# Transformer block on one NeuronCore: the rows of w_down multiplied by the gate g2 beside the up projection, through DRAM

## Chip, cores and metric

The kernel runs on one core of one Trainium2 chip. The metric is the device time of one execution in microseconds. Three runs of the kernel before gave 1492.29, 1489.33 and 1492.66 us; their median is 1492.29 us.

The engines are named as in the profile: PE is the matrix engine, DVE the vector engine, ACT the scalar engine, POOL is GpSimd, and SP is the engine whose queue starts the DMAs of this kernel.

## The reference

One diffusion block over 1024 tokens of width 1024. With `c` the conditioning row, the part that matters here is

```
sh1, sc1, g1, sh2, sc2, g2 = split(silu(c) @ w_mod + b_mod, 6)
h = rms_norm(x, norm1) * (1 + sc1) + sh1
x = x + g1 * (neighbourhood_attention(h, ...) @ w_o)
h = rms_norm(x, norm2) * (1 + sc2) + sh2
a, g = split(h @ w_up, 2)                       # 1024 -> 2 x 2816
x = x + g2 * ((a * gelu(dwconv3(g) + conv_b)) @ w_down)   # 2816 -> 1024
```

The gate `g2` is a row of 1024 numbers, one for each output column. So `g2 * (act @ w_down)` is the same as `act @ (w_down * g2)`, and the kernel uses the second form: every row of `w_down` is multiplied by `g2`, element by element, before it is used. Everything is fp32. Each fp32 matrix product is made of three products of a reduced type: an operand is split into a high part (a copy by ACT) and a low part (the operand minus the high part, by DVE or POOL), and high x high, high x low and low x high are summed.

## The kernel before

Attention and the output projection fill roughly the first 820 us of the span. Behind them come the two stages of the feed-forward part.

**Up projection** (from about 820 to 1240 us). `w_up` and the tokens are cut into 2 x 2 blocks and multiplied in seven products in place of eight. The loop runs over 11 pairs of feature blocks, `i` = 0 to 10, each with `part` 1 (the gate branch `g`, PSUM banks `pg`) and `part` 0 (the value branch `a`, banks `pa`); both share the bank `sw`. Each part has seven steps, `op` in the order 1, 2, 5, 6, 7, 3, 4, so there are 11 x 2 x 7 = 154 steps, and each step is 12 matmuls of 128x512 (line 740). The operand of a step is made ahead of it by `prep_up` (lines 678 to 691): ACT copies the high part (L687) and POOL subtracts it for the low part (L688); this runs `UA` = 6 steps ahead of PE. The raw blocks `ur` come by DMA (L667) and DVE forms their sums (L673 to L675, L686). The banks are emptied by ACT (L772) and DVE (L760, L762, L774, L766); the convolution taps are on DVE (L787). `finish` (L799 to L809) sends the gated rows `y` and four sums of them, `sa` and `sb` (DVE, L804 to L807), to `act_dram`.

**Down projection** (from about 1240 us to the end). It has the same seven products, over 11 blocks `c` in groups of 2, 3, 3 and 3. `load_raw` (L853 to L863) brings two blocks of 128 rows of `w_down` into SBUF as tiles `dr{c}_0` and `dr{c}_1` (L861) and multiplies each by `g2b`, the gate row copied to all partitions: the block with `m` = 0 on POOL, that with `m` = 1 on DVE (L862, 128x1024 each). That makes 22 loads of 512 KB, 11 products on POOL and 11 on DVE. `prep_b` forms the block sums on DVE (L887, L889, L891, L893) and splits the results (ACT L895; POOL or DVE L896). `prep_a` loads the gated rows `da` from `act_dram` (L869) and splits them (ACT L870; POOL or DVE L871). `down_mm` runs the matmuls (L909 to L911) in the banks `dtr`, `dpq`, `dpo` and `dx`, which are the banks that the up projection used, and DVE adds each result to its accumulator (L914). The accumulators start as the residual rows.

**What sets the order.** Each engine executes its instructions in a fixed order, and so does the DMA queue of SP. The program's order is not taken as written: a scheduler orders every engine's instructions by a simulated timeline. It mixes work of the down projection into the end of the up projection: the loads `dr` of group 0 stand on SP's queue ahead of the last `act_dram` stores, and the products and block sums of `dr` stand on POOL and DVE between the splits and taps of the last two feature pairs. `tc.issue_after(x)` holds an instruction back in that order until `x` has been placed, and adds no wait.

**Buffers.** `dr` tiles lie in the eight buffers that the `ur` tiles used (tag x1) and in six others (tag wa). `g2b` is loaded at the end of the first feature pair (L833 to L835), into the buffer of the first `ur` tile.

Of the kernel before, what the change touches and what calls it, by code (L numbers as in the profile page):

```python
# [10 lines left out]
F32 = mybir.dt.float32  # L11
F32R = mybir.dt.float32r
AF = mybir.ActivationFunctionType
ALU = mybir.AluOpType
# [4 lines left out]
P = 128  # L19
D = 1024  # L20
# [10 lines left out]
NF = DFF // P  # L31
# [5 lines left out]
HALF = 512  # L37
# [13 lines left out]
NA = ()  # L51
WD, SQD = range(8), ()
LAG = 1
DG = (1,)
HP_ = (3, 5, 6)
RL = 6
WORD = (1, 2, 5, 6, 7, 3, 4)
DORD = (2, 1, 5, 6, 3, 7, 4)

# [2 lines left out]
def block_kernel(ctx, tc, x, ctxt, cc, w_mod, b_col, b_row, n1, n2, w_qkv, gains, rpb_t, mask_i, mask_r, w_o,  # L62
                 w_up, conv_w, conv_b, w_down, comb, out):
    nc = tc.nc
    PE, ACT, DVE, POOL, SP = nc.tensor, nc.scalar, nc.vector, nc.gpsimd, nc.sync
# [11 lines left out]
    def f(ap):  # L77
        return ap.bitcast(F32)
# [5 lines left out]
    dram = ctx.enter_context(pool("dram", space=DRAM))  # L84
# [22 lines left out]
    o_dram = dram.tile([NPAIR, P, SEQ], F32, name="o_dram")  # L107
    g_dram = dram.tile([2, D], F32, name="g_dram")
    x1_dram = dram.tile([NB, P, D], F32, name="x1_dram")
    act_dram = dram.tile([NF // 2, P, 7, HALF], F32, name="act_dram")  # L110

    big = ctx.enter_context(pool("big", side="right"))
# [43 lines left out]
        DVE.tensor_scalar(ss, ss, 1.0 / D, EPS, ALU.mult, ALU.add)  # L156
        POOL.tensor_tensor(ss, ss, mhalf[:, 0:1], ALU.pow)

    # adaLN of the attention branch, normalised and modulated tokens, transposed and split
    att = ExitStack()  # L160
    sa = att.enter_context(pool("sa"))

# [106 lines left out]
            if si == 3:  # L269
                DVE.tensor_tensor(b1, pc[:, 1], bcol[:, 0:8].unsqueeze(2).broadcast_to([P, KC, 2]), ALU.add)  # L270

    # attention, with the projections of the next pair of heads in between
    sb = att.enter_context(pool("att"))
    mi = sb.tile([P, 3 * P], F32, name="mi")
    SP.dma_start(out=mi, in_=mask_i)
# [179 lines left out]
        DVE.tensor_tensor(res[a:b], po[a:b], tmp[a:b], ALU.add)  # L455
        SP.dma_start(out=o_dram[p, a:b, u * 2 * P:(u + 1) * 2 * P], in_=res[a:b])

    # adaLN of the rest, a little at a time
    def mod_gen():
        order = [2, 3, 4, 5]  # L460
        for sgi in order:
# [27 lines left out]
                        DVE.scalar_tensor_tensor(dst, dst, 1.0, n2c[:, nk * hf:nk * (hf + 1)], ALU.add, ALU.mult)  # L489
                yield  # L490

    # output projection: its first half runs beside the attention of the last heads
    xpool = ctx.enter_context(ExitStack())
    x1, wo, g1b, xsb = {}, [], [], []
    HP = NPAIR // 2
# [106 lines left out]
    filler(10 ** 6)  # L602
    att.close()

    # rest of the output projection, second norm, operands of the Winograd form (seven products of halves
    # in place of eight) of the up projection: A is w_up^T in 2 x 2 blocks, B the tokens in 2 x 2 blocks
    ff = ctx.enter_context(ExitStack())
    usb = ff.enter_context(pool("ffn"))
    BT = {}
    btags = ["bA"] * 12 + ["bB"] * 10 + ["wa"] * 6  # L610
    for i, op in enumerate(WORD):
        for j in range(4):
            tag = btags[4 * i + j]
# [3 lines left out]
            else:  # L617
                BT[op, hl, kk] = usb.tile([P, 2, HALF], F32R, tag=tag, bufs=12 if tag == "bA" else 10,
                                          name=f"b{op}{hl}{kk}")
# [26 lines left out]
            ACT.activation(h, r, AF.Copy)  # L646
            (POOL if op in HP_ else DVE).tensor_tensor(l, r, f(h), ALU.subtract)

    # up projection, gate with the token convolution; the gated rows and their sums go out for the down projection
    NP2 = NF // 2  # L650
    lo_, hi_ = slice(0, HALF), slice(HALF, SEQ)
    uraw, uop = {}, {}
    parts = [(i, part) for i in range(NP2) for part in (1, 0)]
    useq = [(0, 1, 1), (0, 1, 2), (0, 0, 1), (0, 0, 2)] + [(0, part, op) for part in (1, 0) for op in WORD[2:]]
    useq += [(i, part, op) for i, part in parts[2:] for op in WORD]
# [22 lines left out]
    def prep_up(i, part, op):  # L678
        if (i, part) == (0, 1) and op in (1, 2):
            s = xslot(f"u{i}_{part}_{op}", F32R)  # L680
        else:
            s = slot(("rh", "rl")[cnt[0] % 2], f"u{i}_{part}_{op}", shape=(P, 2, HALF))
            cnt[0] += 1
        r = uraw[i, part]
        if op == 3:
            DVE.tensor_tensor(r[3], r[2], r[6], ALU.subtract)  # L686
        ACT.activation(s[:, 0], r[op], AF.Copy)  # L687
        POOL.tensor_tensor(s[:, 1], r[op], f(s[:, 0]), ALU.subtract)  # L688
        uop[i, part, op] = s
        if op == 4 and parts.index((i, part)) + 2 < len(parts):  # L690
            raw_up(*parts[parts.index((i, part)) + 2])
# [107 lines left out]
    def finish(i, y):  # L799
# [8 lines left out]
        SP.dma_start(out=act_dram[i, :, 3:5, :], in_=sa_)  # L808
        SP.dma_start(out=act_dram[i, :, 5:7, :], in_=sb_)  # L809

    sw = ps.tile([P, SEQ], F32, tag="s", bufs=1, name="sw")
    late_p1 = usb.tile([P, HALF], F32, name="late_p1")
    nprep, gens, g, y, late = 2, {}, {}, {}, []
    for k, (i, part, op) in enumerate(useq):
        while nprep < min(k + 1 + UA, len(useq)):
            prep_up(*useq[nprep])
            nprep += 1
        if (i, part) not in gens:
            if part:
                g[i] = [slot("wx", f"g{i}_{m}", F32) for m in range(2)]  # L820
                y[i] = [slot("t4", f"y{i}_{m}", F32) for m in range(2)]
            gens[i, part] = up_part(i, part, g[i] if part else y[i])
        next(gens[i, part])
        if op == WORD[-1]:
            if part:
                for m in range(2):
                    conv(2 * i + m, g[i][m], y[i][m])
                for o, p in late:
                    DVE.tensor_tensor(o, p, o, ALU.mult)
                late.clear()  # L830
            else:
                finish(i, y[i])
                if i == 0:  # L833
                    g2b = slot("gb", "g2b", F32)
                    SP.dma_start(out=g2b, in_=g_dram[1:2, :].broadcast_to([P, D]))  # L835

    # down projection, also in seven products; rows of w_down scaled by the gate g2
    xt = ps.tile([P, 2, HALF], F32, tag="s", bufs=1, name="dx")
    tr = [ps.tile([P, HALF], F32, tag="tr", bufs=3, name=f"dtr{j}") for j in range(3)]
    pq = [ps.tile([P, HALF], F32, tag="pq", bufs=2, name=f"dpq{j}") for j in range(2)]  # L840
# [12 lines left out]
    def load_raw(c):  # L853
        for m in range(2):
            if rt[0] % 14 < 8:
                r = xsb[0].tile([P, D], F32, tag="x1", bufs=NB, name=f"dr{c}_{m}")
            else:
                r = slot("wa", f"dr{c}_{m}", F32)
            rt[0] += 1
            fc = 2 * c + m  # L860
            SP.dma_start(out=r, in_=w_down[fc * P:(fc + 1) * P, :])  # L861
            (DVE if m in DG else POOL).tensor_tensor(r, r, g2b, ALU.mult)  # L862
            raws[c, m] = r  # L863

    def prep_a(q):
# [114 lines left out]
```

## Time and profile before

| quantity | value |
|---|---|
| median of three runs | 1492.29 us (1489.33 to 1492.66) |
| span of the profiled execution | 1491.8 us |
| PE busy | 1386.5 us (93%), 7396 matmuls |
| DVE busy | 1208.1 us (81%) |
| POOL busy | 805.7 us (54%) |
| ACT busy | 738.1 us (49%) |
| moved by DMA | 153.27 MB, 103 GB/s over the span |

The profile is of one execution, for which the trace gives the span, from its first to its last instruction, of 1491.8 us; no separate time of that execution is given, and the span lies 0.5 us below the median of the runs. A row of a group reads: line, engine, operation, tile written <- tiles read, shape, count | busy us, mean ns of one | idle us of its engine just before, and whose end that idle time waited for. A row of the timeline begins with its start and its length in us, and ends with the idle time before it and its releaser in brackets. In a table of stretches, x is the number of instructions, and PEclk the clock that the throttle granted PE, 1.00 being full. Busy shares are averages over stages; which engine is late is read stage by stage.

### The profile page before, as it was taken

The numbers are of one execution on the slowest core, as the hardware profiler recorded it, in microseconds if no ns is written. First come the engines' busy times: TensorE is split into PE (matmuls) and PEld (weight loads), VectorE is DVE, ScalarE is ACT, GpSimd is POOL, SyncE is SP. The second block draws the span as 40 slices with busy tenths as digits, with TensorE's granted clock in tenths as the row PEclk, the third lists the DMA queues.
The fourth block names the chain that finished last, engine by engine and source line by source line (L and its number), as shares of the span: only waits on it lengthen the run. The fifth ranks groups of instructions, "written<-read, shape, count | busy, mean of one in ns | idle before, by whom it ended". The sixth has DMA issues, their size and how long they took to land.

```text
span 1491.8 us, 22077 instructions
## 1 busy us (share of the span) xinstructions
PE 1386.5 (93%) x7396; PEld 1200.0 (80%) x7396; DVE 1208.1 (81%) x2392; ACT 738.1 (49%) x1601; POOL 805.7 (54%) x672
## 2 busy tenths in 40 slices
PE   6689999999999999999996999999999987898998
PEld 2589889898989899888885777888888865686887
DVE  6778878888888878866589889788877779988884
ACT  6575645555565656645465434344343334244541
POOL 1455544545454546744368545555545568474872
PEclk9899999999999999999997999999999998899999
DMA  9612221313131202262132132233332347433343
GB/s 315 161 37 60 64 87 55 92 51 103 49 101 45 77 14 73 69 152 76 50 129 99 64 108 101 96 106 106 107 106 99 106 137 286 155 100 127 110 131 105
DMA packets 84827, 153.27 MB, mean 103 GB/s; under 512 B 9945, under 2 KB 49001, under 8 KB 84713
## 3 DMA queue, kind: packets, MB, share of 16 engines
q1 hardware_dynamic: 84712, 151.86, 32.7%
q8 instruction: 58, 0.95, 0.3%
q14 instruction: 57, 0.46, 0.1%
HBM read 119.05 MB, written 32.78 MB: 102 GB/s over the span
## 4 chain that ended last, share of the span: by engine, by line
PE 60%; DVE 20%; DMA 7%; POOL 5%; issue 4%; ACT 3%; SPq 0%; DVEq 0%; POOLq 0%; ACTq 0%
PE pg L740 8%; PE pa L740 7%; PE sw L740 6%; PE pq L301 5%; PE pq L303 5%; PE pq L305 5%; DMA mr<-in_w_mod_dram 2%; DVE y L787 2%; DVE p L410 2%; POOL u L688 2%; PE s L398 2%; PE po L448 2%; PE po L449 2%; PE py L525 2%; PE py L526 2%
## 5 line engine op out<-in xcount | busy, mean ns | idle before, releaser
L688 POOL TENSOR_TENSOR u<-ur,u 128x512 fp32r<-128x512 f32 x154 | 231.9, 1519 | 176.8 <-ACT u L687 175.1
L417 POOL TENSOR_TENSOR p<-p,m 128x640 f32<-128x640 f32 (+1 forms) x128 | 157.3, 1230 | 157.0 <-DVE m L413 116.0
L301 PE MATMUL pq<-wh,hth 128*128 128x384 f32 (+1 forms) x640 | 219.7, 343 | 17.1 <-DVE kn L340 15.3
L305 PE MATMUL pq<-wh,htl 128*128 128x384 f32 (+1 forms) x640 | 215.2, 336 | 2.4 <-DVE htl L194 1.4
L303 PE MATMUL pq<-wl,hth 128*128 128x384 f32 (+1 forms) x640 | 215.0, 336 | 0.5 <-POOL wl L147 0.5
L687 ACT ACTIVATE u<-ur 128x512 fp32r<-128x512 f32 x154 | 93.9, 628 | 116.1 <-PE sw L740 45.4
L412 ACT ACTIVATE p<-p,m 128x640 f32<-128x640 f32 (+1 forms) x128 | 102.9, 804 | 84.3 <-DVE m L410 75.2
L301 PEld LDWEIGHTS pq<-wh,hth 128*128 128x128 f32 x640 | 124.8, 195 | 23.1 <-DVE kn L340 9.2
L325 POOL TENSOR_TENSOR qss<-qss,mhalf 128x4 f32<-128x4 f32 (+1 forms) x80 | 79.9, 999 | 97.0 <-DVE qss L324 82.8
L305 PEld LDWEIGHTS pq<-wh,htl 128*128 128x128 f32 x640 | 124.7, 195 | 3.2 <-DVE htl L194 3.2
L303 PEld LDWEIGHTS pq<-wl,hth 128*128 128x128 f32 x640 | 124.8, 195 | 1.6 <-issue 0.9
L787 DVE SCALAR_TENSOR_TENSOR y<-g,cw,y 128x896 f32<-128x896 f32 (+1 forms) x132 | 102.8, 842 | 19.2 <-ACT y L781 19.1
L449 PE MATMUL po<-pt,v 128*128 128x256 f32 x352 | 93.3, 293 | 2.1 <-DVE pt L437 2.1
L448 PE MATMUL po<-pt,v 128*128 128x256 f32 x352 | 93.8, 289 | 0.1
L895 ACT ACTIVATE db<-dr 128x512 fp32r<-128x512 f32 x77 | 47.4, 629 | 87.3 <-PE dx L911 55.7
L871 POOL TENSOR_TENSOR da<-da 128x512 fp32r<-128x512 f32 x44 | 74.9, 1725 | 27.4 <-ACT da L870 27.4
L896 POOL TENSOR_TENSOR db<-dr,db 128x512 fp32r<-128x512 f32 x44 | 64.9, 1494 | 45.6 <-ACT db L895 34.3
L410 DVE CUSTOM_DVE_ANT_0 p<-s,bias 128x640 f32<-128x640 f32 x96 | 78.3, 816 | 9.5 <-PE s L399 8.9
L436 ACT ACTIVATE pt<-pl 128x384 fp32r<-128x384 f32 (+1 forms) x128 | 58.0, 461 | 47.6 <-PE pl L429 46.6
L471 DVE SCALAR_TENSOR_TENSOR macc<-mr,cs,macc 128x256 f32<-128x256 f32 x112 | 65.0, 581 | 13.9 <-DMA mr<-in_w_mod_dram 13.0
L437 DVE TENSOR_TENSOR pt<-pl,pt 128x384 fp32r<-128x384 f32 (+1 forms) x128 | 65.4, 516 | 6.7 <-ACT pt L436 6.2
L449 PEld LDWEIGHTS po<-pt,v 128*128 128x128 f32 x352 | 66.6, 189 | 4.0 <-DVE pt L437 3.4
(258 smaller groups left out, 4184.3 us busy)
## 6 DMA issues: line engine op xcount, KB each, us to landing
ur<-in_w_up_dram SPq DMA_DIRECT2D x44, 512.0 KB
da<-act_dram SPq DMA_DIRECT2D x77, 256.0 KB
mr<-in_w_mod_dram SPq DMA_DIRECT2D x128, 128.0 KB
dr<-in_w_down_dram SPq DMA_DIRECT2D x22, 512.0 KB
wraw<-in_w_qkv_dram SPq DMA_DIRECT2D x56, 192.0 KB
mraw<-in_w_mod_dram SPq DMA_DIRECT2D x16, 512.0 KB
act_dram<-sa SPq DMA_DIRECT2D x11, 512.0 KB
act_dram<-y SPq DMA_DIRECT2D x11, 512.0 KB
```

The source lines that it names most:

```text
L301: PE.matmul(pq[:, c0:], hth[t][:, k, :], wh[:, c0:], start=(k == 0), stop=False)
L303: PE.matmul(pq[:, c0:], hth[t][:, k, :], wl[:, c0:], start=False, stop=False)
L305: PE.matmul(pq[:, c0:], htl[t][:, k, :], wh[:, c0:], start=False, stop=(k == KC - 1))
L410: DVE.tensor_tensor_reduce(out=dst, in0=src, in1=bb, scale=1.0, scalar=3e38, op0=ALU.add, op1=ALU.min, accum_out=m[:, 0:1])
L412: ACT.activation(w[:, :n], w[:, :n], AF.Exp, bias=m[:, 0:1], scale=-1.0, accum_out=m[:, 1:2])
L417: POOL.tensor_tensor(w[:, :n], w[:, :n], m[:, 2:3].broadcast_to([P, n]), ALU.mult)
L448: PE.matmul(po, v, th[:, j].rearrange("p a b -> p (a b)"), start=(m == 0), stop=False)
L449: PE.matmul(po, v, tl[:, j].rearrange("p a b -> p (a b)"), start=False, stop=(m == len(blks) - 1))
L687: ACT.activation(s[:, 0], r[op], AF.Copy)
L688: POOL.tensor_tensor(s[:, 1], r[op], f(s[:, 0]), ALU.subtract)
L740: PE.matmul(bank, a, b, start=(start and k == 0 and n == 0), stop=(k == 3 and n == 2), skip_group_check=True)
L787: DVE.scalar_tensor_tensor(o, i, w, o, ALU.mult, ALU.add)
```

## The change

The 22 products at L862 go away. In their place the new helper `gate_w` handles 44 halves of 128x512: it loads a half block of `w_down` into a new tile `wg` (two buffers), multiplies it by its half of `g2b` on POOL, and stores it in a new DRAM tensor `wg_dram`. One `gate_w` is called every third step of the up projection from step 16 on, so the calls are at steps 16, 19, ..., 145 of 0 to 153. Its POOL instruction is held, by `issue_after`, behind the low-part split `lo_ins` that the same step issued. `load_raw` loads the finished rows from `wg_dram`, 512 KB each as before, and issues no product. The products on DVE are gone (`DG` is removed). The bytes moved grow by the 11.5 MB that are stored, since w_down is read once as before and the finished rows are read once more (another 11.5 MB).

```
-DG = (1,)
+G0 = 16
+    wg_dram = dram.tile([NF, P, D], F32, name="wg_dram")
...
-        POOL.tensor_tensor(s[:, 1], r[op], f(s[:, 0]), ALU.subtract)
+        lo_ins[:] = [POOL.tensor_tensor(s[:, 1], r[op], f(s[:, 0]), ALU.subtract)]
...
+    def gate_w(n):
+        fc, hf = divmod(n, 2)
+        c = slice(hf * HALF, (hf + 1) * HALF)
+        r = usb.tile([P, HALF], F32, tag="wg", bufs=2, name=f"wg{n}")
+        SP.dma_start(out=r, in_=w_down[fc * P:(fc + 1) * P, c])
+        with tc.issue_after(lo_ins[0].ins):
+            POOL.tensor_tensor(r, r, g2b[:, c], ALU.mult)
+        SP.dma_start(out=wg_dram[fc, :, c], in_=r)
...
         next(gens[i, part])
+        if k >= G0 and (k - G0) % 3 == 0 and (k - G0) // 3 < 2 * NF:
+            gate_w((k - G0) // 3)
...
-            SP.dma_start(out=r, in_=w_down[fc * P:(fc + 1) * P, :])
-            (DVE if m in DG else POOL).tensor_tensor(r, r, g2b, ALU.mult)
+            SP.dma_start(out=r, in_=wg_dram[fc])
```

The following rows are pieces of the engines' orders. Lines above 809 of the new file stand one line lower for the same code (L688 is L689 there), and lines of the down projection twelve lower (L887 is L899). The number in `u9_0_7` is feature pair, part and step.

POOL near the end of the up projection, before; `dr0_0` and `dr1_0` are the first two blocks of the down projection:

```order
L688 TENSOR_TENSOR u9_0_3_13105<-ur9_0_0_12855,u9_0_3_13105 128x512
L688 TENSOR_TENSOR u9_0_7_13089<-ur9_0_1_12857,u9_0_7_13089 128x512
L862 TENSOR_TENSOR dr0_0_13536<-dr0_0_13536,g2b_10702 128x1024
L688 TENSOR_TENSOR u9_0_4_13138<-ur9_0_1_12857,u9_0_4_13138 128x512
L688 TENSOR_TENSOR u10_1_1_13166<-ur10_1_0_12995,u10_1_1_13166 128x512
L688 TENSOR_TENSOR u10_1_2_13183<-ur10_1_0_12995,u10_1_2_13183 128x512
L688 TENSOR_TENSOR u10_1_5_13199<-ur10_1_2_12999,u10_1_5_13199 128x512
L688 TENSOR_TENSOR u10_1_6_13215<-ur10_1_2_12999,u10_1_6_13215 128x512
L862 TENSOR_TENSOR dr1_0_13542<-dr1_0_13542,g2b_10702 128x1024
```

The same place after:

```order
L819 TENSOR_TENSOR wg38_13242<-wg38_13242,g2b_10703 128x512
L689 TENSOR_TENSOR u9_0_7_13246<-ur9_0_1_12998,u9_0_7_13246 128x512
L689 TENSOR_TENSOR u9_0_3_13262<-ur9_0_0_12996,u9_0_3_13262 128x512
L689 TENSOR_TENSOR u9_0_4_13295<-ur9_0_1_12998,u9_0_4_13295 128x512
L819 TENSOR_TENSOR wg39_13323<-wg39_13323,g2b_10703 128x512
L689 TENSOR_TENSOR u10_1_1_13327<-ur10_1_0_13144,u10_1_1_13327 128x512
L689 TENSOR_TENSOR u10_1_2_13344<-ur10_1_0_13144,u10_1_2_13344 128x512
L689 TENSOR_TENSOR u10_1_5_13360<-ur10_1_2_13148,u10_1_5_13360 128x512
L819 TENSOR_TENSOR wg40_13376<-wg40_13376,g2b_10703 128x512
```

The two products of 128x1024 are gone from here, and a product of 128x512 stands behind every third split; this pattern fills POOL's order from the 16th step on.

DVE where the rows of feature pair 9 are finished, before; L766 is the gating product, L887 the first block sum of the down projection:

```order
L762 TENSOR_TENSOR tmp9_0_13152<-tmp9_0_13152 128x512
L887 TENSOR_TENSOR dr1_0_13542<-dr1_0_13542 128x512
L766 TENSOR_TENSOR y9_1_13006<-tmp9_0_13152,y9_1_13006 128x512
L762 TENSOR_TENSOR tmp9_0_13152<-pa9_1_13150,tmp9_0_13152 128x512
L766 TENSOR_TENSOR y9_0_13005<-tmp9_0_13152,y9_0_13005 128x512
L862 TENSOR_TENSOR dr1_1_13545<-dr1_1_13545,g2b_10702 128x1024
L804 TENSOR_TENSOR sa9_13270<-y9_0_13005,y9_1_13006 128x512
L806 TENSOR_TENSOR sb9_13271<-y9_0_13005 128x512
```

The same place after:

```order
L899 TENSOR_TENSOR dr1_0_13717<-dr1_0_13717 128x512
L775 TENSOR_TENSOR tmp9_0_13309<-sw_10403,tmp9_0_13309 128x512
L763 TENSOR_TENSOR tmp9_0_13309<-tmp9_0_13309 128x512
L767 TENSOR_TENSOR y9_1_13155<-tmp9_0_13309,y9_1_13155 128x512
L763 TENSOR_TENSOR tmp9_0_13309<-pa9_1_13307,tmp9_0_13309 128x512
L767 TENSOR_TENSOR y9_0_13154<-tmp9_0_13309,y9_0_13154 128x512
L805 TENSOR_TENSOR sa9_13439<-y9_0_13154,y9_1_13155 128x512
L807 TENSOR_TENSOR sb9_13440<-y9_0_13154 128x512
```

The product L862 is gone from between the gating and the sums; the block sum (now L899) stays in DVE's order, two places earlier, and waits for the load of `dr1_0` itself.

SP's queue at the same time, before:

```order
L861 DMA dr1_0_13542<-in_w_down_dram 128x1024
L800 DMA act_dram_86<-y9_0_13005 128x512
L861 DMA dr1_1_13545<-in_w_down_dram 128x1024
L861 DMA dr2_0_13644<-in_w_down_dram 128x1024
L808 DMA act_dram_86<-sa9_13270 128x1024
L801 DMA act_dram_86<-y9_1_13006 128x1024
L809 DMA act_dram_86<-sb9_13271 128x1024
L869 DMA da0_2_13560<-act_dram_86 128x512
```

The same place after:

```order
L820 DMA wg_dram_86<-wg41_13433 128x512
L874 DMA dr2_0_13817<-wg_dram_86 128x1024
L817 DMA wg43_13556<-in_w_down_dram 128x512
L820 DMA wg_dram_86<-wg42_13503 128x512
L809 DMA act_dram_87<-sa9_13439 128x1024
L802 DMA act_dram_87<-y9_1_13155 128x1024
L810 DMA act_dram_87<-sb9_13440 128x1024
L874 DMA dr2_1_13819<-wg_dram_86 128x1024
L874 DMA dr3_0_13821<-wg_dram_86 128x1024
L820 DMA wg_dram_86<-wg43_13556 128x512
L874 DMA dr3_1_13823<-wg_dram_86 128x1024
```

The last loads and stores of `wg` stand between the `dr` loads and the stores of `act_dram`, and the first load of gated rows, `da0_2`, which followed `sb9` directly, now follows `dr3_1` and one accumulator load.

## Prediction before the run

> **What bounds the kernel now.** I read the table of stretches first, because PE is busy for 93% of the span and only the stretches in which it is not can give anything back. The table covers one window of the steady up projection, the two windows in which the up projection hands over to the down projection, and a later one that also falls short.
>
> ```profile
> core 0: us, PE busy (x) PEld busy (x) DVE busy (x) ACT busy (x) POOL busy (x), PEclk, DMA share, GB/s
> 1000.00:1060.00 60.00, 60.00 (x259) 48.46 (x258) 52.12 (x60) 23.89 (x38) 30.25 (x21) 1.00 0.34 114
> 1120.00:1180.00 60.00, 60.00 (x259) 48.45 (x259) 46.70 (x56) 21.18 (x34) 30.93 (x22) 1.00 0.33 112
> 1200.00:1240.00 40.00, 34.39 (x146) 26.75 (x145) 31.59 (x35) 15.06 (x24) 23.09 (x13) 1.00 0.52 175
> 1240.00:1300.00 60.00, 46.90 (x171) 35.71 (x170) 58.13 (x61) 18.86 (x34) 44.52 (x21) 0.86 0.64 227
> 1340.00:1360.00 20.00, 14.45 (x59) 10.85 (x58) 16.14 (x19) 8.29 (x14) 14.60 (x9) 0.97 0.45 150
> 1400.00:1440.00 40.00, 40.00 (x178) 33.13 (x177) 36.10 (x45) 20.74 (x34) 25.27 (x17) 1.00 0.36 113
> ```
>
> In the up projection PE is never idle: 60.00 us for 259 matmuls, 0.2317 us each. At that rate the 146 matmuls from 1200 to 1240 need 33.8 us, so 6.2 us are lost there; the 171 from 1240 to 1300 need 39.6 us, so 20.4 us are lost, part of it to a clock of 0.86; the 59 from 1340 to 1360 need 13.7 us, so 6.3 us are lost. DVE is busy for 58.13 of the 60 us in the second of these: there DVE sets the pace.
>
> The list of PE's waits from 1176 to 1300 says the same; its columns are the waiting group, what it waited for, us in total, times, longest.
>
> ```profile
> PE dpq L909 <- DVE acc L914: 4.8, 2, 4.0
> PE dpq L909 <- DVE tmp L762: 4.3, 1, 4.3
> PE pg L740 <- ACT tmp L772: 3.2, 1, 3.2
> PE dtr L909 <- ACT db L895: 2.6, 1, 2.6
> PE sw L740 <- DVE g L760: 1.5, 1, 1.5
> ```
>
> Most of it ends on DVE. The groups of DVE from 1240 to 1300, and the waits of DVE and POOL over the whole handover, show what the products at L862 do there.
>
> ```profile
> L862 DVE TENSOR_TENSOR dr<-dr,g2b 128x1024 f32<-128x1024 f32 x5 | 8.3, 1650 | 0.0
> ...
> DVE dr L887 <- POOL dr L862: 5.6, 2, 3.9
> DVE da L871 <- ACT da L870: 3.0, 2, 2.9
> DVE dr L862 <- DMA dr<-in_w_down_dram: 1.3, 1, 1.3
> ...
> POOL dr L862 <- DMA dr<-in_w_down_dram: 14.4, 5, 5.3
> ```
>
> **Term 1: the handover.** All 22 products leave the down projection. From 1240 to 1300 that takes 8.3 us of DVE's own work away. It takes away POOL's products too, and these slow DVE, as the timeline shows: three DVE operations beside three POOL products, and below them the same shape and line with POOL idle.
>
> ```profile
> 1265.30 8.34 POOL L862 TENSOR_TENSOR dr<-dr,g2b 128x1024 f32<-128x1024 f32 x3
> ...
> 1266.41 2.25 DVE L804 TENSOR_TENSOR sa<-y,y 128x512 f32<-128x512 f32 x1
> 1268.58 2.85 DVE L806 TENSOR_TENSOR sb<-y 128x512 f32<-128x512 f32 x1
> 1271.36 2.82 DVE L766 TENSOR_TENSOR y<-tmp,y 128x512 f32<-128x512 f32 x1
> ...
> 1048.31 0.69 DVE L804 TENSOR_TENSOR sa<-y,y 128x512 f32<-128x512 f32 x1
> 1049.52 1.78 DVE L805 TENSOR_TENSOR sa<-sa,y 128x512 f32<-128x512 f32 x1
> ```
>
> The three take 7.92 us where three times 0.69 us would do: 5.9 us. So DVE's work falls from 58.1 to 58.1 - 8.3 - 5.9 = 43.9 us, and PE needs 39.6. The stretch can shrink by up to 16 us before another bound holds it. POOL's splits of `da` and `db` stay, DVE's block sums stay, and they now wait for the loads themselves; I allow 4 us for that, near the 5.6 us that DVE's block sums waited for POOL's products, and take **-12**. The ends are -20.4 (PE loses nothing any more) and -5 (DVE keeps being late in another place, and only the longest of the waits, 4.8 us, goes).
>
> From 1200 to 1240 DVE is not full, and the 6.2 us come from waits. The 3.2 us wait is for ACT, which waits for the buffer that DVE's gating product frees; that product stands behind a block sum that waits for POOL's L862, which waits for its load. In the new order no product stands there. I take **-3**, with ends 0 and -6.2. The first loads of gated rows are issued later (behind `wg43` and `dr3_1`), but `da0_2` is used only after the taps of pair 10 in the new DVE order, where before DVE sat 3.0 us for it.
>
> **Term 2: the third group's last block.** At 1354 the same chain stands alone.
>
> ```profile
> 1350.27 0.33 SPq L861 DMA_DIRECT2D dr<-in_w_down_dram  x1
> 1354.07 2.35 POOL L862 TENSOR_TENSOR dr<-dr,g2b 128x1024 f32<-128x1024 f32 x1 [0.86 <-DMA dr<-in_w_down_dram]
> 1356.45 1.73 DVE L887 TENSOR_TENSOR dr<-dr 128x512 f32<-128x512 f32 x1 [3.86 <-POOL dr L862]
> 1358.84 0.71 PE L909 MATMUL dx<-db,da 128*128 128x512 f32 x1 [4.69 <-DVE acc L914]
> ```
>
> The block sum of `dr10_0` keeps its place in DVE's order, ahead of the accumulation that PE waits for. Without the product it starts when the load lands, 2.35 us earlier; POOL's other product, that of `dr9_0`, is also gone ahead of it, so the split that frees the buffer and lets the load start comes about as much earlier. Together that is the 4.69 us. I take **-5**, with the slow matmuls behind the wait counted in; ends 0 and -6.3, the whole loss there.
>
> **Term 3: the products in the up projection.** 44 products of 128x512 join POOL's splits, which have the same shape.
>
> ```profile
> L688 POOL TENSOR_TENSOR u<-ur,u 128x512 fp32r<-128x512 f32 x86 | 125.1, 1464 | 115.7 <-ACT u L687 115.5
> L766 DVE TENSOR_TENSOR y<-tmp,y 128x512 f32<-128x512 f32 x25 | 25.9, 1034 | 0.6
> L675 DVE TENSOR_TENSOR ur<-ur,ur 128x512 f32<-128x512 f32 x13 | 16.6, 1278 | 0.0
> ...
> DVE ur L673 <- POOL u L688: 10.6, 8, 1.7
> ...
> L862 POOL TENSOR_TENSOR dr<-dr,g2b x11: 2347/2417/2857, 1182.2 to 1354.1; 128x1024 f32<-128x1024 f32 x11
> L862 DVE TENSOR_TENSOR dr<-dr,g2b x11: 1208/1214/3408, 1192.0 to 1363.5; 128x1024 f32<-128x1024 f32 x11
> ```
>
> These rows are of 940 to 1180, 240 us, except the last two, which are of the whole run. POOL idles 115.7 us there; 44 products of 1.46 us are 64 us over some 360 us, in which it idles about 173. So POOL has the room. DVE pays: L766 and L675 take (1034 - 690) x 25 + (1278 - 690) x 13 = 16 us more beside 86 splits than at the free 690 ns of that shape, 0.19 us a split, so 44 products add at least 8 us of DVE time in the stage; at most each one lengthens one operation by 1.1 us (1.78 against 0.69), 48 us. PE shows no wait in these windows, so DVE's free time covers the first figure. What is not covered is a product in front of a split on which DVE then waits: 8 of 86 splits are such, so 4 of 44 products, 6 us, and behind L673 stand the bank emptyings that PE needs. I take a third, **+2**, with ends 0 and +6; more than that is the third rival.
>
> A product at L862 takes 2417 ns on POOL and 1214 ns on DVE. The Trainium skill, GPSIMD Engine Reference, section 3.1 ("Elementwise — side-by-side cycle accounting"), says that a two-input elementwise operation is about twice as slow there and belongs on the vector engine; the factor agrees (1.99), and by that rule the change is a loss of engine time, 40 us of products becoming 64. It costs only if POOL's idle time does not hold it. The Trainium skill, SBUF — State Buffer, section "Who interferes with whom", says that a DVE operation with two SBUF inputs and a GpSimd operation block each other for a whole instruction. By that, a product costs DVE up to its own 1.46 us, 64 us in all in place of 48, and DVE would be near full, which leads to the third rival and its 1505 us; the row with 1.78 against 0.69 shows 1.1.
>
> **SP's queue.** A store of `wg` waits for its product, and behind it on SP wait the `ur` loads and the `act_dram` stores; the load two products later waits until that store has landed. Two rows of the chain and timeline price that.
>
> ```profile
> 1223.67 5.15 DMA dr<-in_w_down_dram
> ...
> 1158.71 4.47 SPq L667 DMA_DIRECT2D ur<-in_w_up_dram  x2
> ...
> 1175.89 0.69 DVE L673 TENSOR_TENSOR ur<-ur 128x512 f32<-128x512 f32 x1 [1.68 <-POOL u L688]
> ```
>
> A 512 KB load took 5.15 us, so a store and a load of half that take at most 10.3; six steps of 12 x 0.2317 us are 16.7. So the next load is in time with 6 us to spare. A pair of `ur` loads was issued from 1158.71 to 1163.18 and first read at 1175.89, where DVE waited for POOL and not for the load: some 7 us to spare. Cost nothing; if that cover goes, POOL waits with splits behind it, and PE still has six steps, 16.7 us, of finished operands.
>
> **The sum.** -12 - 3 - 5 + 2 = -18. The profiled span is 1491.8 us, which is 0.5 below the median, so the median should go to 1491.8 - 18 + 0.5 = **1474.3 us**. No change of under 0.2%, 3 us, can be told from none.
>
> **Rivals.**
> *Everything comes back.* PE loses nothing in the handover and in the last block: -20.4 - 6.2 - 6.3 + 2 = -31, 1461 us. For it: DVE's 43.9 us are near PE's 39.6. Against: the first operands of the down projection still need the gated rows of the up projection, and the 2.6 us wait for ACT's `db` has no product in its chain. Chance 0.12.
> *Another wait takes the place.* Only the chains with L862 in them shorten (3.2 + 4.7 us, less 2), and DVE stays late behind POOL's splits, on which it waits already: -6, 1486 us. For it: POOL is busy for 44.5 of 60 us there. Chance 0.17.
> *The up projection slows.* Every third split has a product in front of the next; where DVE's L673 stands behind it, the emptying of bank `sw` (L774) comes late and PE stops. It decides the sign at 20 / 44 = 0.45 us of PE for each product; if half of the products cost PE their whole 1.5 us, that is 33 - 20 = +13, 1505 us. For it: DVE at 52.12 of 60 from 1000 to 1060; 7 products there at 1.1 us make it 59.8. Against: PE has not one wait in this window, and POOL's idle time lies between the splits. It is also where the rule of the SBUF page would lead. Chance 0.13.
> That the products do not move is excluded: no L862 is left in the new order.
>
> **Chances.** The forecast, 0.58, with its own range of 1466 to 1483. The range of 1463 to 1490 leaves out about half of the first rival (0.06) and most of the third (0.11). Faster: 0.58 + 0.12 + 0.10 of the second = 0.80. Same: 0.07 + 0.03 of the third = 0.10. Slower: 0.10.
>
> **What would show it.** Right: DVE clearly below 58 of 60 us in the handover, its L804 and L806 there near 0.69 us, PE's 4.69 us wait gone, PE at 60.00 of 60 between 1000 and 1180. Wrong: PE waits on DVE in the up projection, or POOL waits for the loads of `wg` there; or the handover loses as much as now, with waits on POOL's splits or on loads from `wg_dram`.

## The result and the profile after

The kernel after takes 1499.89 us in the median of 4 runs (1498.20 to 1501.47), the kernel before 1490.81 us (1488.18 to 1492.66) beside it. The ratio is 1.0055, with a 95% interval of 1.0037 to 1.0074: slower by 0.55%. The forecast was 1474.3 us, faster by 1.2%; it was wrong, in sign too. The profiled execution of the kernel after has a span of 1499.3 us, against 1491.8. It moved 176.35 MB by DMA, against 153.27: the bytes grew by 23.1 MB, which are the stored rows and the same rows read back; the 11.5 MB named in the section on the change are half of that.

Lines of the kernel after have numbers higher by 1 than those of before up to L808 (L688 is now L689, L762 is L763); the products are L819, and the matmuls of the down projection L921 to L923. The table of stretches of the kernel after, with the columns as in the prediction:

```profile
1000.00:1060.00 60.00, 57.37 (x242) 44.63 (x241) 57.43 (x60) 24.30 (x37) 39.50 (x26) 1.00 0.40 136
1120.00:1180.00 60.00, 54.18 (x223) 42.55 (x222) 51.31 (x53) 21.80 (x32) 38.20 (x26) 0.97 0.39 136
1200.00:1240.00 40.00, 38.27 (x164) 30.37 (x163) 34.07 (x34) 15.87 (x25) 27.03 (x18) 1.00 0.44 150
1240.00:1300.00 60.00, 51.80 (x202) 40.53 (x201) 51.09 (x65) 22.76 (x38) 30.55 (x20) 0.91 0.79 288
1340.00:1360.00 20.00, 20.00 (x90) 16.58 (x89) 14.07 (x20) 9.76 (x16) 14.40 (x11) 1.00 0.51 168
```

The last three rows have what the forecast hoped for: 164, 202 and 90 matmuls where there were 146, 171 and 59. The first two have the loss: 242 and 223 matmuls in 60 us of the up projection where there were 259. Longer stretches make the sum. The same view of the kernel before:

```profile
900.00:1180.00 280.00, 279.93 (x1203) 225.68 (x1203) 231.39 (x277) 112.41 (x173) 144.83 (x100) 1.00 0.31 105
1180.00:1300.00 120.00, 101.29 (x400) 78.58 (x400) 106.94 (x114) 41.22 (x67) 79.69 (x41) 0.93 0.52 183
1300.00:1440.00 140.00, 134.45 (x583) 109.78 (x582) 119.66 (x147) 64.13 (x104) 92.29 (x60) 0.99 0.36 113
```

and of the kernel after:

```profile
900.00:1180.00 280.00, 261.03 (x1087) 204.50 (x1086) 243.51 (x250) 102.67 (x157) 187.59 (x122) 0.99 0.44 151
1180.00:1300.00 120.00, 110.07 (x450) 87.06 (x449) 104.49 (x119) 44.24 (x72) 72.21 (x47) 0.96 0.62 222
1300.00:1440.00 140.00, 140.00 (x619) 115.94 (x619) 116.27 (x151) 67.34 (x109) 84.66 (x59) 1.00 0.40 128
```

From 900 to 1180 there are 116 matmuls fewer, at 280 / 1203 = 0.2327 us each **27.0 us lost**. From 1180 to 1300 there are 50 more, 11.6 us at 0.2317; from 1300 to 1440 36 more, 8.1 us at 140 / 619 = 0.2262: **19.7 us gained**. That leaves 7.3 us lost, of the 7.5 us by which the spans differ. The stretches are cut by the clock, so that from 1180 on the kernel after is still at earlier work. Cut by work, the picture is the same: the last matmuls of the up projection start at 1275.5 us in place of 1256.5, 19.0 us later, and from there to the end the kernel after takes 11.5 us less.

The list of PE's waits from 900 to 1180, which was empty before, names the banks:

```profile
PE sw L741 <- DVE tmp L763: 8.5, 7, 2.5
PE pa L741 <- ACT tmp L773: 6.4, 5, 2.3
PE sw L741 <- DVE tmp L775: 2.3, 1, 2.3
PE pg L741 <- ACT g L773: 1.6, 2, 1.1
```

PE waits until DVE and ACT have emptied `sw`, `pa` and `pg`. ACT's copies at L773 (L772 before) are themselves held up by DVE's gating product, before and after:

```profile
ACT tmp L772 <- DVE y L766: 9.7, 3, 5.1
ACT tmp L773 <- DVE y L767: 26.6, 6, 8.8
```

PE is idle for 19.0 of the 27.0 us. The other 8 us are matmuls that took longer, 261.03 / 1087 = 0.2401 us of busy time each in place of 0.2327. Part of that is the clock: behind the longest wait, which ends at 947.97, PE was granted 0.55 and 0.59 for 4 us. The rest was not taken apart.

```profile
948.00:950.00 2.00, 2.00 (x5) 1.61 (x6) 2.00 (x4) 0.85 (x2) 0.00 (x0) 0.55 0.33 131
950.00:952.00 2.00, 2.00 (x7) 1.55 (x6) 1.52 (x3) 0.74 (x2) 1.66 (x1) 0.59 0.96 316
```

The timeline shows how the longest wait, of 2.50 us, comes about.

```profile
935.57 1.75 POOL L689 TENSOR_TENSOR u<-ur,u 128x512 fp32r<-128x512 f32 x1
936.20 1.67 DVE L767 TENSOR_TENSOR y<-tmp,y 128x512 f32<-128x512 f32 x1
937.28 1.75 POOL L819 TENSOR_TENSOR wg<-wg,g2b 128x512 f32<-128x512 f32 x1
937.97 0.69 DVE L763 TENSOR_TENSOR tmp<-pa,tmp 128x512 f32<-128x512 f32 x1
...
938.99 3.79 POOL L689 TENSOR_TENSOR u<-ur,u 128x512 fp32r<-128x512 f32 x3
...
941.57 1.77 DVE L687 TENSOR_TENSOR ur<-ur,ur 128x512 f32<-128x512 f32 x1 [2.90 <-POOL u L689]
942.75 1.73 POOL L819 TENSOR_TENSOR wg<-wg,g2b 128x512 f32<-128x512 f32 x1
943.26 1.77 DVE L767 TENSOR_TENSOR y<-tmp,y 128x512 f32<-128x512 f32 x1
944.44 1.72 POOL L689 TENSOR_TENSOR u<-ur,u 128x512 fp32r<-128x512 f32 x1
945.07 1.65 DVE L805 TENSOR_TENSOR sa<-y,y 128x512 f32<-128x512 f32 x1
...
947.24 0.68 DVE L763 TENSOR_TENSOR tmp<-sw,tmp 128x512 f32<-128x512 f32 x1
...
947.97 0.61 PE L741 MATMUL sw<-b7h,u 128*128 128x512 f32 x1 [2.50 <-DVE tmp L763]
```

GpSimd now has work without a gap from 935.57 to 946.2: splits and two products. Each DVE operation with both inputs in SBUF that falls beside it takes 1.65 to 1.77 us in place of 0.68 (L767, L687, L767, L805). L763, which reads a PSUM bank, keeps its 0.69 us even beside a product, but in DVE's order it stands behind those, and PE stands behind it. In the same chain DVE also stood idle for 2.90 us until a split had ended, with a product in front of the splits. So this picture alone does not separate the longer operations from the later splits; the run `a6_fill_beside` does.

The size of it for the whole stage: DVE was busy for 231.39 us in 1203 matmuls before and for 243.51 us in 1087 after, 0.1923 and 0.2240 us for each. There is a product at every third step, that is every 36 matmuls, so a product costs DVE (0.2240 - 0.1923) x 36 = **1.14 us** of busy time, though it does not run on DVE.

### The profile page after: what moved, and what is told of

It reads as the page before. It is cut to its first block, busy times and chain, and to the rows that moved or that the text cites. A ratio compares the mean times of both kernels' runs of the same rounds, so it can differ in the third digit from the quotient of the medians.

```text
span 1499.3 us, 22256 instructions
## 1 busy us (share of the span) xinstructions
PE 1387.9 (93%) x7396; PEld 1198.5 (80%) x7396; DVE 1223.2 (82%) x2381; ACT 737.4 (49%) x1601; POOL 844.5 (56%) x705
## 2 busy tenths in 40 slices
DMA packets 97499, 176.35 MB, mean 118 GB/s; under 512 B 11352, under 2 KB 50408, under 8 KB 97384
## 5 line engine op out<-in xcount | busy, mean ns | idle before, releaser
L689 POOL TENSOR_TENSOR u<-ur,u 128x512 fp32r<-128x512 f32 x154 | 239.8, 1571 | 146.6 <-ACT u L688 132.3
L688 ACT ACTIVATE u<-ur 128x512 fp32r<-128x512 f32 x154 | 92.6, 627 | 92.5 <-PE sw L741 41.6
L788 DVE SCALAR_TENSOR_TENSOR y<-g,cw,y 128x896 f32<-128x896 f32 (+1 forms) x132 | 116.4, 946 | 19.2 <-ACT y L782 19.2
L883 POOL TENSOR_TENSOR da<-da 128x512 fp32r<-128x512 f32 x44 | 67.8, 1564 | 30.0 <-ACT da L882 29.9
L741 PE MATMUL sw<-b7h,u 128*128 128x512 f32 x176 | 61.6, 409 | 10.1 <-DVE tmp L763 9.7
```

The costliest lines, as they stand in the source:

```text
L689: lo_ins[:] = [POOL.tensor_tensor(s[:, 1], r[op], f(s[:, 0]), ALU.subtract)]
L741: PE.matmul(bank, a, b, start=(start and k == 0 and n == 0), stop=(k == 3 and n == 2), skip_group_check=True)
L788: DVE.scalar_tensor_tensor(o, i, w, o, ALU.mult, ALU.add)
```

## The experiments

The theory that I took to the chip: GpSimd's products lengthen DVE's operations beside them, and the loss is theirs. Rivals: the transfers on SP's queue; the delay of GpSimd's splits; the new order that the scheduler made.

**Four parts taken alone.** `a1_no_gate` is the kernel before without its 22 products; its output lacks the gate:

```diff
-            (DVE if m in DG else POOL).tensor_tensor(r, r, g2b, ALU.mult)
```

> The kernel before with the 22 products of w_down with g2 left out (its output lacks the gate); nothing is added to the up projection. It prices what the down projection gains by losing them. By the sum of losses in the kernel after, 1200 to 1300 and 1340 to 1360 get back 11.4 + 6.3 = 17.7 us: about 1473 us, with PE at 60.00 of 60 from 940 to 1180. If the handover's gain in the kernel after came only from a later start of the down projection and not from the missing products, this run stays within 5 us of 1491.

Measured: 1466.19 us, ratio 0.9831 (0.9818 to 0.9844), 25.9 us less than the 1492.04 of the kernel before beside it. Its table:

```profile
900.00:1180.00 280.00, 279.93 (x1204) 226.03 (x1203) 231.36 (x277) 112.61 (x173) 144.42 (x100) 1.00 0.31 105
1180.00:1300.00 120.00, 113.02 (x482) 91.34 (x481) 95.42 (x131) 48.94 (x79) 55.96 (x37) 0.97 0.56 196
1300.00:1440.00 140.00, 139.30 (x615) 115.09 (x614) 114.03 (x141) 67.09 (x108) 99.51 (x68) 1.00 0.39 123
```

82 matmuls more in the handover (19.0 us) and 32 more behind it (7.2 us) are the gain, more than the 17.7 us expected. The products do cost the down projection that much, and the kernel after got 11.6 of the 19.0 us.

`a2_copy_only` is the kernel after without its 44 products, with the transfers; its output lacks the gate:

```diff
-        with tc.issue_after(lo_ins[0].ins):
-            POOL.tensor_tensor(r, r, g2b[:, c], ALU.mult)
```

> The kernel after with GpSimd's 44 products left out (its output lacks the gate); the loads of wg, the stores and the detour through DRAM stay. Theory: the products themselves slow the up projection, so without them PE is back at 60.00 of 60 from 940 to 1180 and the time is about 1473 us. Rival 1, the queue: the 88 transfers on SP's queue delay the loads of ur and the stores of act_dram, and most of the 26 us stays: about 1497 us. Rival 2, the order: the scheduler's new order of PE and DVE costs it; then the time lies between, 1480 to 1497 us, as far as this kernel's order is still that of the kernel after.

Measured: 1471.20 us, ratio 0.9855 (0.9837 to 0.9872). So the kernel after is 1499.9 - 1471.2 = 28.7 us slower with its 44 products than without them. The first line is the stage, the second the loads of the tile `wg`:

```profile
900.00:1180.00 280.00, 279.92 (x1204) 225.75 (x1203) 233.53 (x276) 110.80 (x171) 151.57 (x102) 1.00 0.31 105
```

```profile
L817 SPq DMA_DIRECT2D wg<-in_w_down_dram x44: 327/333/1697, 749.0 to 894.3; - x44
```

PE is full again from 900 to 1180, but the run says less on the queue than it was meant to: with no product to wait for, all 44 loads and stores were issued by 897.5. The transfers do not run beside the steady up projection here. The 5.0 us to `a1_no_gate` are what the burst costs elsewhere: from 820 to 900 PE made 299 matmuls, and 324 in `a1_no_gate`. So the 28.7 us, too, compare two places of the transfers, and are not a clean price of the products. What the queue costs in the up projection is read from the next run.

`a3_products_beside` adds the products alone to the kernel before, without transfers:

```diff
...
+    def gate_w(n):
+        c = slice(n % 2 * HALF, (n % 2 + 1) * HALF)
+        with tc.issue_after(lo_ins[0].ins):
+            POOL.tensor_tensor(wg[n % 2], wg[n % 2], g2b[:, c], ALU.mult)
...
```

> The kernel before, complete, with 44 more products of 128x512 on GpSimd, at the same steps of the up projection as in the kernel after, on two resident tiles whose result nobody reads; no transfer is added, and the down projection is unchanged. Theory: the up projection loses the same 26 us as in the kernel after: about 1517 us. Rival 1, the queue: no transfer, no loss: 1491 us. Rival 2, the order: between 1491 and 1517 us, as the scheduler places DVE's and PE's instructions here.

Measured: 1525.14 us, ratio 1.0222 (1.0209 to 1.0236), 33.1 us above the kernel before; 1517 were expected.

```profile
900.00:1180.00 280.00, 263.48 (x1099) 206.84 (x1098) 243.75 (x253) 103.76 (x159) 191.99 (x125) 0.99 0.27 94
```

104 matmuls fewer, 24.2 us, without a single added transfer. Of the 27.0 us that the kernel after loses in this stage 2.8 are left for the queue and for the different order. The rest of the 33 us is lost outside the stage, some 2 us before 900 (315 matmuls from 820 to 900 in place of 323) and the others behind 1180, where the products at L862 are still there. The queue is out as the main cause.

`a4_products_dve` puts the 44 products on DVE:

```diff
-            POOL.tensor_tensor(r, r, g2b[:, c], ALU.mult)
+            DVE.tensor_tensor(r, r, g2b[:, c], ALU.mult)
```

> The kernel after with the 44 products on DVE in place of GpSimd. A two-input operation of 128x512 takes DVE 0.69 us when GpSimd is idle, so this adds 30 us to DVE in the up projection in place of up to 48, and no split of GpSimd stands behind a product. Theory: the loss shrinks to a third or less, about 1473 + 9 = 1482 us. Rival 1, the queue: the transfers are the same, so about 1497 us. If DVE's share is what counts, whichever engine multiplies, 52 of 60 become 57 and the time stays at 1490 or above.

Measured: 1492.93 us, ratio 1.0009 (0.9999 to 1.0019): a gain of 7 us on the kernel after, less than half of what I expected. The stage, and DVE's longest wait from 900 to 1180:

```profile
900.00:1180.00 280.00, 268.39 (x1127) 214.09 (x1126) 226.88 (x287) 105.37 (x161) 148.94 (x96) 0.98 0.44 149
```

```profile
DVE wg L819 <- DMA wg<-in_w_down_dram: 25.6, 11, 4.1
```

76 matmuls fewer, 17.7 us, but DVE is less busy than before (226.88 against 231.39 us): it waited 25.6 us for the loads of `wg`. With two buffers a load starts only when the product two places before it has been stored. The scheduler had moved all 44 products ahead, into the time from 832 to 1014 us, and DVE, which came to them in quick succession, stood there with the bank emptyings behind it; from 1020 to 1180 PE lost nothing (690 matmuls in 160 us). I take this loss for a wait and not for DVE's work, which `a5_dve_spaced` tests.

**GpSimd's time or its reads.** `a6_fill_beside` is `a3_products_beside` with each product replaced by two fills, which keep GpSimd as long without reading; against that run:

```diff
...
-            POOL.tensor_tensor(wg[n % 2], wg[n % 2], g2b[:, c], ALU.mult)
+            POOL.memset(wg, 0.0)
+            POOL.memset(wg[:, lo_], 0.0)
```

> The run a3_products_beside with each product replaced by two fills with zero on GpSimd, of 128x1024 and 128x512 (0.53 us or more for 128x512 in that run, so 1.6 us or more for the two): GpSimd is kept from its splits as long, but reads nothing from SBUF; the kernel is complete. Theory 1, the products' reads lengthen DVE's operations with two inputs in SBUF: DVE keeps its 0.191 us for each matmul and the time stays within 8 us of the kernel before, 1492 to 1500 us. Theory 2, the products delay GpSimd's splits and what waits for them: about 1525 us, as with products. Theory 3, the scheduler's new order of DVE and PE, which is changed in as many rows as with products: about 1525 us too.

Measured: 1491.93 us, ratio 0.9997 (0.9983 to 1.0012). The stage, and GpSimd's groups in it:

```profile
900.00:1180.00 280.00, 278.97 (x1198) 224.34 (x1196) 236.15 (x274) 113.10 (x175) 191.25 (x166) 1.00 0.30 103
```

```profile
L818 POOL MEMSET wg<- 128x1024 f32 x33 | 31.4, 952 | 0.0
L819 POOL MEMSET wg<- 128x512 f32 x33 | 17.4, 526 | 1.0
```

This decides it. GpSimd is busy for 191.25 us, as with the products (191.99), and the two fills hold it for 1.48 us where a product took 1.57. DVE waited as long for GpSimd's splits, 9.8 us in the stage against 10.2 with the products, and DVE's order differs from that of the kernel before in some 350 rows in both runs; yet PE makes 1198 matmuls. The delay of the splits and the scheduler's order cost at most 5 matmuls, 1.2 us. What costs is that the products read SBUF. The Trainium skill, SBUF — State Buffer, section "Who interferes with whom", says just this: an operation of DVE with two inputs in SBUF contends with a GpSimd instruction that reads SBUF, not with one that only writes it. The two runs agree with it, 24.2 us against 1.2.

**How much of it.** `a7_half_beside` is `a3_products_beside` with half of the products; against that run:

```diff
-        if k >= G0 and (k - G0) % 3 == 0 and (k - G0) // 3 < 2 * NF:
-            gate_w((k - G0) // 3)
+        if k >= G0 and (k - G0) % 6 == 0 and (k - G0) // 6 < NF:
+            gate_w((k - G0) // 6)
```

> The run a3_products_beside with 22 products, one at every sixth step, in place of 44 at every third; the kernel is complete. With 44, DVE was busy for 2.67 us of each step of 2.78 us; with 22 it should be 2.48. Theory 1a, DVE's full share makes the loss: with a tenth of its time free the loss is at most a quarter of 33 us, 1492 to 1500 us. Theory 1b, each product costs PE the same, 0.75 us: 1492 + 16.5 = 1508 us.

Measured: 1503.40 us, ratio 1.0069 (1.0051 to 1.0086), 11.4 us above the kernel before: between the two theories, and in the range of neither.

```profile
900.00:1180.00 280.00, 276.45 (x1181) 220.93 (x1180) 235.80 (x267) 110.92 (x168) 174.24 (x116) 1.00 0.29 99
```

In this stage 22 matmuls are missing, 5.1 us, a fifth of the 24.2, with half of the products: there the loss is not proportional. DVE pays (235.80 / 1181 - 0.1923) x 72 = 0.53 us for a product, half as much as with twice as many, and PE loses 5.1 / 17 = 0.30 us for each of the 17 products of the stage, against 24.2 / 31 = 0.78. The other 6 us are lost outside it, and were not taken apart.

`a8_four_pieces` cuts the products of the kernel after:

```diff
-            POOL.tensor_tensor(r, r, g2b[:, c], ALU.mult)
+            for q in range(4):
+                a, b = q * P, (q + 1) * P
+                POOL.tensor_tensor(r[:, a:b], r[:, a:b], g2b[:, hf * HALF + a:hf * HALF + b], ALU.mult)
```

> The kernel after, complete, with each product cut into four of 128x128, one behind the other on GpSimd. The run a6_fill_beside showed that what GpSimd reads is what costs. Theory 1, an operation of DVE waits until the operation of GpSimd beside it has ended: it now waits for a piece of some 0.4 us in place of 1.57 us, so the 28.7 us of the products fall to a third to a half: about 1471 + 10 to 15 = 1481 to 1486 us. Theory 2, the two share the reads at a lower rate for as long as both read: cutting changes nothing, about 1500 us, more if the four pieces together take GpSimd longer.

Measured: 1492.73 us, ratio 1.0007 (0.9995 to 1.0019): 7 us better than uncut, half of what Theory 1 expected at least, and so between the two theories. The stage, GpSimd's pieces by duration (minimum, median, maximum), and three DVE operations beside four pieces in the timeline:

```profile
900.00:1180.00 280.00, 270.44 (x1146) 213.65 (x1145) 239.17 (x262) 108.10 (x166) 224.75 (x221) 1.00 0.46 155
```

```profile
L821 POOL TENSOR_TENSOR wg<-wg,g2b x126: 447/628/1333, 901.0 to 1179.5; 128x128 f32<-128x128 f32 x126
```

```profile
1017.06 3.52 POOL L821 TENSOR_TENSOR wg<-wg,g2b 128x128 f32<-128x128 f32 x4
1017.69 0.83 DVE L805 TENSOR_TENSOR sa<-y,y 128x512 f32<-128x512 f32 x1
1018.45 0.95 DVE L807 TENSOR_TENSOR sb<-y 128x512 f32<-128x512 f32 x1
1019.32 0.94 DVE L806 TENSOR_TENSOR sa<-sa,y 128x512 f32<-128x512 f32 x1
```

The same operations took 1.78 us beside a split of 128x512; beside pieces they take 0.83 to 0.95. So DVE waits for the end of one operation of GpSimd, and a shorter one costs it less: for the single operation that is Theory 1. In the stage the loss falls from 116 matmuls to 57. But four pieces take GpSimd 4 x 0.72 = 2.9 us in the mean in place of 1.57, it is busy for 224.75 of 280 us, and DVE waited 15.8 us for its splits in the stage, against 10.3 in the kernel after. That is where I see the rest, without having tested it.

**The version that follows.** If DVE does not wait for its loads, its own product should be cheaper for it than GpSimd's. `a5_dve_spaced` loads one product ahead into a third buffer, stores one later, and ties the product to the bank emptying of its step:

```diff
...
+    def gate_w(n):
+        if n:
+            gate_store(n - 1)
+        else:
+            gate_load(0)
+        if n + 1 < 2 * NF:
+            gate_load(n + 1)
+        hf = n % 2
+        with tc.issue_after(put_ins[0].ins):
+            DVE.tensor_tensor(wgt[n], wgt[n], g2b[:, hf * HALF:(hf + 1) * HALF], ALU.mult)
...
```

> The kernel after, complete, with the 44 products on DVE, each loaded one product ahead into a third buffer (shared with late_p1), issued behind the bank emptying of its own step, and stored one product later. In the run a4_products_dve DVE waited 25.6 us for the loads of wg between 900 and 1180, and its loss lay there, before 1060. If that wait is its whole loss, DVE now pays 0.7 to 0.9 us for a product, 0.3 us a step of 12 matmuls, 2.55 us of the step's 2.78, and the time is 1471.2 + 2 to 8 = 1473 to 1480 us. If DVE's work itself costs PE, whatever it waits for, it stays near 1493 us.

Measured: 1477.65 us, ratio 0.9893 (0.9875 to 0.9911), within the 1473 to 1480 expected.

```profile
900.00:1180.00 280.00, 277.70 (x1189) 222.56 (x1188) 242.56 (x301) 112.25 (x169) 153.68 (x100) 1.00 0.48 161
1180.00:1300.00 120.00, 108.24 (x452) 85.61 (x451) 102.98 (x140) 46.86 (x74) 51.76 (x33) 0.97 0.66 230
```

14 matmuls are missing in the stage, 3.3 us, with the transfers of all products running beside it. A product on DVE took 1.08 us in the mean, but DVE as a whole pays (242.56 / 1189 - 0.1923) x 36 = 0.42 us for it, since other operations now fall beside fewer splits: L676 takes 0.76 us in place of 1.27 (L675 before), and 4 of 14 run beside a GpSimd operation in place of 11 of 15. DVE no longer waits for a load. The run changed two things at once, though: the products are also spread over 374 us, from 866 to 1240, where they filled 182 us in `a4_products_dve`. Which of the two returned how much was not separated.

`a9_dve_earlier` is `a5_dve_spaced` with the products ended ahead of the handover:

```diff
-        if k >= G0 and (k - G0) % 3 == 0 and (k - G0) // 3 < 2 * NF:
-            gate_w((k - G0) // 3)
+        if k >= G0 and (k - G0) % 5 in (0, 2) and (k - G0) // 5 < NF:
+            gate_w((k - G0) // 5 * 2 + (k - G0) % 5 // 2)
```

> The run a5_dve_spaced, complete, with two products in every five steps in place of one in every three, so that the last product comes at step 123 of 153 in place of step 145, ahead of the handover. There a5_dve_spaced still made 452 matmuls from 1180 to 1300 where a2_copy_only made 486, 7.9 us. Theory 1, these 7.9 us are the last products and their transfers beside the handover: it returns most of them, and the up projection pays one or two us more, so about 1472 us. Rival, DVE has no more room in the up projection: twelve products in thirty steps where ten were cost PE more than the handover returns, 1478 us or above.

Measured: **1470.10 us, ratio 0.9859 (0.9842 to 0.9877)**, the fastest complete kernel of the study, 1.4% ahead of the kernel before and 30 us ahead of the kernel after.

```profile
900.00:1180.00 280.00, 278.59 (x1197) 224.26 (x1196) 253.46 (x311) 113.97 (x173) 156.68 (x100) 1.00 0.52 175
1180.00:1300.00 120.00, 112.39 (x474) 89.03 (x473) 99.15 (x133) 49.36 (x78) 54.48 (x37) 0.99 0.56 198
```

The handover makes 474 matmuls, 22 more than in `a5_dve_spaced`, and the up projection has not lost by it, with DVE busy for 253.46 of 280 us. So a DVE that is 91% busy keeps PE at 1197 matmuls here, and one that is 87% busy in the kernel after does not: the busy share of DVE does not tell whether PE waits; which operations are late does.

## Why the prediction was wrong, point by point

**Term 1, the handover (-15): right in cause and place.** Without the products the handover returns 19.0 us (`a1_no_gate`), within the ends. The kernel after got 11.6. Its own last products ran into the handover, the last one at 1251.7; that these cost the difference is shown only for products on DVE, where `a9_dve_earlier`, which ends them at 1163.5, gets 74 matmuls, 17.1 us, and `a5_dve_spaced` 52. DVE's 43.9 us from 1240 to 1300 were not reached (51.09 after, 50.70 in `a1_no_gate`): PE made 202 and 226 matmuls there in place of 171, and so brought DVE its next work. One sign of being right showed only in part: L804 (L805 after) still took 1.74 us there once, beside a split on GpSimd.

**Term 2, the third group's last block (-5): right.** PE is busy for 20.00 of 20 us, and the 4.69 us wait is gone. The whole stretch from 1300 to 1440 gave 8.1 us, above the end of 6.3. That terms 1 and 2 add up to 19.7 us, where 20 were forecast, is luck in part: the one gave 3.4 less, the other 3.1 more.

**Term 3, the products in the up projection (+2, ends 0 and +6): this is the step that failed.** The stage lost 27.0 us in the kernel after and 24.2 with the products alone; over the whole kernel the products cost 28.7 (`a2_copy_only`) to 33.1 us (`a3_products_beside`). Two parts of the term were wrong. First the price of a product to DVE: the 0.19 us a split was worked out from two of DVE's lines alone. Others are lengthened as much, in the same profile of the kernel before, from 900 to 1180:

```profile
L686 DVE TENSOR_TENSOR ur<-ur,ur 128x512 f32<-128x512 f32 x15 | 16.9, 1128 | 1.2 <-POOL u L688 1.2
L806 DVE TENSOR_TENSOR sb<-y 128x512 f32<-128x512 f32 x7 | 8.1, 1155 | 0.0
```

The same working over all eleven groups of 128x512 with their inputs in SBUF gives 44.6 us beside 100 splits, 0.45 us a split, and with the taps at L787, every operation counted against the shortest of its line and shape, 0.66. So the splits already cost DVE more than three times the price taken. The other bound, 1.1 us, was in the text, and the measured figure is 1.14: a product fills a gap of GpSimd in which DVE ran undisturbed, and 30 of the 31 products of the stage overlap a lengthened DVE operation, where before 76 of 99 splits did. Second the cover: "PE shows no wait in these windows, so DVE's free time covers the first figure". That PE never waits says that the emptyings come in time, not by how much. Of DVE's 48.6 us of idle time from 900 to 1180, 14.8 lie in front of the taps and 10.6 in front of L673, where it waits for ACT and GpSimd. The late operations lie elsewhere: ahead of the longest wait, in the run of L767, L687 and L805 in front of the emptying of `sw`. The waits for a split, which I priced, did not even grow. That of L673 (L674 after) is 10.6 us before and 5.8 after; with that of L686 (L687 after), 1.2 and 4.5 us, the sums are 11.8 and 10.3:

```profile
DVE ur L674 <- POOL u L689: 5.8, 4, 1.7
DVE ur L687 <- POOL u L689: 4.5, 2, 2.9
```

**SP's queue (nothing): right within some 3 us in the up projection**, by `a3_products_beside` against the kernel after, whose orders are not quite the same. GpSimd waited once for a load of `wg`, 1.8 us. The burst of `a2_copy_only` shows that the same transfers cost 5 us when bunched ahead of it.

**The third rival is what happened.** Its place (bank `sw`) and its point of decision (0.45 us of PE for each product) hold: 27.0 us for the 31 products of the stage are 0.87. Its 1505 us lie 5 above the result. The mechanism it named was another, a product in front of a split on which DVE waits; what happened is that DVE's operations beside the product take longer. That POOL's idle time lies between the splits was counted against it and was the reason for it: while GpSimd is idle, DVE's operations take 0.69 us, and that time was already in use.

**The rule of the Trainium skill, SBUF — State Buffer**, named there with 64 us of DVE, pointed the right way; the measured 44 x 1.14 = 50 us lie between the row's 48 and it. The prediction told the rule too widely: it holds against a GpSimd operation that reads SBUF, and the fills of `a6_fill_beside` show that the condition counts.

## What to carry to other kernels

Idle time of GpSimd is not free where DVE works on two inputs in SBUF: price a GpSimd operation that reads SBUF as its own length on DVE, until a run shows less, and ask which bank emptying stands behind it. To see what GpSimd's operations cost DVE already, go over all of DVE's lines and not over two. A full PE without waits shows that a stage has no loss, never how much room it has; the room is read from the order of DVE between two emptyings. Moving the products out of the crowded handover was right here; what made it pay was to run them on DVE, whose time they take either way, spread out, with each load issued one product ahead and the last product done before the handover.

## What the runs showed of the hardware

How long a DVE operation of 128x512 with both inputs in SBUF takes follows the length of the GpSimd operation beside it: 0.68 us alone, up to 0.95 in the rows beside 128x128 (0.45 us at its shortest), up to 1.78 beside 128x512, and up to 2.85 beside 128x1024 (2.35 us at its shortest). These are the long ones of the rows shown; the longest of all from 820 to 1260 are 1.00 beside pieces (`a8_four_pieces`) and 1.84 beside 128x512 (the kernel after). The shortest product of 128x512 is in its row of the kernel after:

```profile
L819 POOL TENSOR_TENSOR wg<-wg,g2b x31: 1278/1732/1755, 901.1 to 1178.8; 128x512 f32<-128x512 f32 x31
```

So the addition is 0.27, 1.10 and 2.17 us, each 0.18 us less than the GpSimd operation's own 0.45, 1.28 and 2.35, which fits a wait for one whole operation. GpSimd waits in turn; its product goes from 1.28 to 1.73 us in the median. DVE's operations that read a PSUM bank took 0.67 to 0.71 us before, after and with the products alone. Two fills on GpSimd, 1.48 us together, cost DVE (236.15 / 1198 - 0.1923) x 36 = 0.17 us, where a product cost it 1.14.
